# Block 0 of a bias-GELU MLP: a third pair of h columns by seven block products instead of eight

## The chip, the cores and the metric

The kernel runs on one core of a Trainium2 chip. The metric is device time in microseconds (us); "before" is a median of 875.78 us over 3 runs (875.62 to 875.81).

## The reference

```python
x  = (16, 512, 768)   # float32; taken as 8192 rows of 768
w1 = (768, 3072); b1 = (3072,); w2 = (3072, 768)
y = np.matmul(x, w1) + b1
y = 0.5 * y * (1.0 + erf(y / np.sqrt(2.0)))
return np.matmul(y, w2).astype(np.float32)
```

Two matrix products with a GELU between them. The kernel multiplies in bf16 and accumulates in fp32.

## The kernel before, in words

**Tiling.** The 8192 rows are taken in blocks of 2 x 384 rows (`pairs`; the last block is 2 x 256). The 3072 hidden columns are 24 chunks `hc` of 128. Chunk j and chunk 12 + j form pair j (j = 0 to 11). For each block the kernel makes `g = gelu(x w1 + b1)` in SBUF, one 128-column chunk of each half block at a time, and then the second product from `g`.

**First product, two ways.** `plain(hc, half)` (L407) makes one chunk of one half block with 6 matmuls 128x384 (L414); a pair has two chunks and two halves, so 24 matmuls. `product1` (L149) makes a pair with seven block products P1 to P7 of 3 matmuls each (L158), 21 in all, in the manner of Strassen and Winograd. It multiplies sums of blocks of w1 (seven forms per pair: two are copies of raw blocks, five are sums) with sums of blocks of x (`sum_x`, L296). Between the products VectorE and ScalarE work on the accumulators: after P1 a copy on ScalarE to a second bank, after P7 a copy to the buffer `v`, after P2 and after P6 a subtraction on VectorE (L114), and four GELUs on ScalarE (L146).

**The forms of w1.** `form_w1` (L400, through `make_w1`, L361) makes the forms of the next pair in the order `order1` = 4, 5, 3, 0, 1, 2, ...: a copy on ScalarE (L104) and four VectorE sums (L111, L114). They are kept in staging areas and later stored to DRAM (`w1f`), from which every later block loads them. In block 0 only pairs 4 and 5 are made by products; their forms are read where they were staged. All other pairs of block 0 are plain.

**Second product.** `part2` (L227, matmuls at L233) multiplies 128x128 blocks of `g` with forms of w2 (15 per chunk c of w2, c = 0 to 7) for 15 products M0 to M14 of 8 matmuls each, by groups of three row tiles (G0 and G1 in a block). `load_w2(c)` loads the six raw blocks of a chunk, and `make_w2(c)` (L331, from `w2_sums`, L314) makes the nine sums with six VectorE instructions, in place in `w2t[:, c]`. Sums of `g` that some products need are made by `gsum` (L191) on VectorE; `finish2` (L243) adds or copies each finished product from PSUM to `ot`.

In block 0 the second product of G0 starts with six products that need no sum of `g` (`raws`, L712), chunk by chunk: M4, M14, M13, M8, M7, M6 for c = 0, then for c = 1, up to c = 7. After them `middle` runs M12, M2, M1, M5, M3, M10, M9, M11, then M0. M5 needs a `gsum` of its own, made on VectorE just before. M4, M12, M10 and M11 share a PSUM bank (`BANK`): M11 adds to what M10 left, so it starts when VectorE has read M10's result.

**Borrowed space.** In block 0 the sums of x (`x0f`, L96) lie in `w2t[:, 7]` and the buffers `v` and `u` of the products (`ev0`, L97) lie in `w2t[:, 6]`. So `load_w2(6)` and `load_w2(7)` (L577) stand behind block 0's last product.

**What orders the work.** The order on every engine is the order of the program (`inorder`). VectorE's instructions are placed by hand between the TensorE steps, and each engine executes its own in order. Loads with conversion go through GpSimd's queue (`nc.gpsimd`): x tiles, w1 and w2 in the order in which they are written, with eight in flight (the ninth waits for the first). The next block's x tiles are loaded behind the w2 chunks on the same queue, and transposed from SyncE's queue (L294).

**The start and the end.** Before the first products TensorE runs matmuls on a zeroed tile (`busy`, L423) and transposes six tiles of x (`turn_x0`, L439). At the very end the last row tile is finished by three stretches of output columns (L761): 384, 192 and 192, each followed by a copy on ScalarE and a store from SyncE's queue.

Of the kernel before, what the change touches and what calls it, by code (L numbers as in the profile page):

```python
# [12 lines left out]
P = 128  # L13

W1F = {"P7": 0, "P1": 1, "P2": 2, "P3": 3, "P4": 4, "P6": 5, "P5": 6}
# [18 lines left out]
def kernel(  # L34
# [16 lines left out]
    HP = HC // 2  # L51
    KH = KC // 2
    NB = N // 2
    HW = 384
    QC = HC // 3
    QH = QC // 2
    SLOT = 7 * KH * P
# [7 lines left out]
    while r < R:  # L65
        w = min(HW, (R - r) // 2)
# [8 lines left out]
    def inorder(ins):  # L75
        return tc.keep_in_program_order(ins)
# [10 lines left out]
    w2t = keep.tile([P, QC, NF, NB], BF16, name="w2t")  # L87
# [14 lines left out]
    def copy(engine, dst, src):  # L102
        if engine == "act":
            inorder(nc.scalar.copy(out=dst, in_=src))  # L104
        elif engine == "dve":
            inorder(nc.vector.tensor_copy(out=dst, in_=src))  # L106
        else:
            inorder(nc.gpsimd.tensor_copy(out=dst, in_=src))

    def add(dst, a, b):  # L110
        inorder(nc.vector.tensor_tensor(out=dst, in0=a, in1=b, op=ALU.add))  # L111

    def sub(dst, a, b):
        inorder(nc.vector.tensor_tensor(out=dst, in0=a, in1=b, op=ALU.subtract))  # L114
# [14 lines left out]
    staged = {}  # L129
# [9 lines left out]
    def moving1(m, kc, w, xs):  # L139
        if m in XRAW:  # L140
            kh, half = XRAW[m]
            return xt[:, kh * KH + kc, half, :w]
        return xs[:, XF[m], kc, :w]
# [5 lines left out]
    def product1(t, m, p, j, w):  # L149
        if m == "P1":  # L150
            t["c12"] = bank()
        elif m == "P7":
            t["c22"] = bank()
        ps = t[{"P1": "c12", "P4": "c12", "P7": "c22", "P5": "c22"}.get(m, "c11")]
        at, xs, es = (staged[j], x0f, ev0) if p == 0 else (where[index(p, j)], xft, ev)
        forms = at.rearrange("p (f kc c) -> p f kc c", f=7, kc=KH)
        for kc in range(KH):
            inorder(nc.tensor.matmul(  # L158
                out=ps[:, :w], lhsT=forms[:, W1F[m], kc, :], rhs=moving1(m, kc, w, xs),
                start=(kc == 0 and m in ("P1", "P7")), stop=(kc == KH - 1),  # L160
                skip_group_check=True))
        ps = ps[:, :w]
        v, u = es[:, j % 2, :w], es[:, 2 + j % 2, :w]
        if m == "P1":
            t["c11"] = bank()
            copy("act", t["c11"][:, :w], ps)
        elif m == "P7":
            copy("dve", v, ps)
        elif m == "P2":
            sub(t["c22"][:, :w], ps, v)  # L170
        elif m == "P6":
            sub(u, ps, v)
        elif m == "P4":
            gelu1(HP + j, 0, ps, w, 1.0)
        elif m == "P3":
            if p > 0 and index(p, j) in places:
                fill_slot(places[index(p, j)])
            gelu1(j, 0, ps, w, 1.0)
        elif m == "P5":
            gelu1(j, 1, u, w, -1.0)  # L180
            gelu1(HP + j, 1, ps, w, -1.0)
# [128 lines left out]
    def load_w2(c):  # L310
        h, q = divmod(c, QH)
        dma(nc.gpsimd, out=w2t[:, c, 0:6, :].rearrange("p (k f) n -> p k (f n)", k=3), in_=w2r[:, h, q, :, :])
# [18 lines left out]
    def make_w2(c):  # L331
        for s in w2_sums(c):
            s()
# [17 lines left out]
    def raw(j):  # L351
        c0 = (j % 3) * P
        return w1_pair(j // 3).rearrange("p (b kc c) -> p b kc c", b=4, kc=KH)[:, :, :, c0:c0 + P]
# [4 lines left out]
    order1 = (4, 5, 3, 0, 1, 2, 6, 7, 8, 10, 11, 9)  # L358
    waiting = []

    def make_w1():  # L361
        nonlocal made
        n = made
        made += 1
        j = order1[n]
        a = raw(j)
        area, o = stage[n]
        s = area[:, o:o + SLOT].rearrange("p (f kc c) -> p f kc c", f=7, kc=KH)
        copy("act", s[:, 0:2], a[:, 1:3])

        def one():
            add(s[:, 2], a[:, 1], a[:, 2])
            add(s[:, 3:5], a[:, 0:4:2], a[:, 1:4:2])

        def two():
            sub(s[:, 5], a[:, 2], a[:, 0])
            sub(s[:, 6], a[:, 1], a[:, 3])
            if n < 4:
                waiting.append(lambda queue: dma(queue, out=w1f[j], in_=area[:, o:o + SLOT]))
            else:  # L380
                dma(nc.sync if n < 6 else nc.gpsimd, out=w1f[j], in_=area[:, o:o + SLOT])
            formed.add(j)
            staged[j] = area[:, o:o + SLOT]
            if j in DIRECT:
                where[seq.index(j)] = area[:, o:o + SLOT]

        return one, two
# [12 lines left out]
    def form_w1():  # L400
        for f in make_w1():
            f()
        free_slots()
# [3 lines left out]
    def plain(hc, half, k0=0, k1=KC):  # L407
        if k0 == 0:
            halfway[hc, half] = bank()
        py = halfway[hc, half]  # L410
        h, j = divmod(hc, HP)
        lhs = w1_group(j // 3 * 2 + h)
        for kc in range(k0, k1):
            inorder(nc.tensor.matmul(out=py[:, :HW], lhsT=lhs[:, kc, (j % 3) * P:(j % 3 + 1) * P],  # L414
                                     rhs=xt[:, kc, half, :], start=(kc == 0), stop=(kc == KC - 1)))
        if k1 == KC:
            gelu1(hc, half, py[:, :HW], HW, 1.0)
# [5 lines left out]
    def busy(n):  # L423
        for _ in range(n):
            inorder(nc.tensor.matmul(out=pw[:], lhsT=warm[:, 0:P], rhs=warm, start=True, stop=True))
# [77 lines left out]
    EARLY = ("M2a", "M3a")  # L503
# [3 lines left out]
    tb = turns[1][:, 448:448 + HC]  # L507
    inorder(nc.tensor.transpose(out=tb, in_=b1s, identity=ident32[:HC, :HC]))
    copy("act", b1t[:], tb)
    busy(2)  # L510
    copy("dve", xb0[:, 0, :], xw[:, 0, :])
    turn_x0(0, "dve")
    copy("act", xb0[:, 1, :], xw[:, 1, :])
    busy(1)
    turn_x0(1, "dve")
    busy(1)
    turn_x0(2, "dve")
# [18 lines left out]
    def plains(gi):  # L536
        for n in range(3):
            hc = gi % 2 * HP + gi // 2 * 3 + n
            plain(hc, 0)
            plain(hc, 1)  # L540

    blk = groups(0)
# [9 lines left out]
    form_w1()  # L552
    plain(3, 1)
    plain(HP + 3, 0)
    t0 = {4: dict(), 5: dict()}
    c0 = w2_sums(0)

    def step0(j, *ms):
        for m in ms:
            product1(t0[j], m, 0, j, HW)  # L560
# [13 lines left out]
    step0(5, "P4", "P6", "P5")  # L574
    plain(6, 0)
    step0(5, "P3")
    for c in (QC - 2, QC - 1):  # L577
        load_w2(c)
    for f in c0:
        f()  # L580
    form_w1()
    make_w2(1)
    plain(6, 1)
    for hc in (7, 8):
        plain(hc, 0)
        plain(hc, 1)
    for m in EARLY:
        gsum(blk[0], m)
    form_w1()
    make_w2(2)  # L590
    make_w2(3)
    make_w2(4)
    plains(5)
    for m in MIDDLE[:2]:
        gsum(blk[0], m)
    make_w2(5)
    make_w2(6)
    plains(6)
    plains(7)
    make_w2(7)  # L600
    for m in ("M1", "M3b", "M10a", "M10b", "M11a", "M11b"):
# [27 lines left out]
    for p, (r0, w) in enumerate(pairs):  # L629
        nxt = pairs[p + 1] if p + 1 < len(pairs) else None  # L630
        G0, G1 = blk
        blk = groups(p + 1) if nxt is not None else None
# [100 lines left out]
        if full:  # L733
            run(take(9))
            if p == 0:
                form_w1()
            for m in ("M14", "M8", "M4"):
                rest(G1, m)
            if p > 0:
                for k in range(4):  # L740
                    sum_x(k, nxt[1])
            for m in ("M7", "M6", "M13"):
                rest(G1, m)
            if p == 0:
                form_w1()
            at = {5: (0,), 6: (1,), 7: (2,)} if p == 0 else {}
            middle(G1, lambda n: [lambda k=k: sum_x(k, nxt[1]) for k in at.get(n, ())])
            if p > 0:
                ahead(p + 1)
            rest(G1, "M0")  # L750
            if p == 0:
                sum_x(3, nxt[1])
        else:
            a = lambda k: block(G1, 0, k)
            d12, d13 = st[:, 4, :, :], st[:, 5, :, :]
            sub(d12, a(0), a(1))
            sub(d13, a(0), a(2))
            t = ot[:, G1["o"][2], :]
            halves = ((("b31", a(2)), ("M4", a(1)), ("b11", d12)), (("M13", a(2)), ("b22", a(1)), ("b12", d13)))
            rows = of[G1["rows"][0]:G1["rows"][0] + P, :]  # L760
            for n, c0, c1 in ((0, 0, NB), (1, 0, NB // 2), (1, NB // 2, NB)):  # L761
                terms = halves[n]
                ps = bank()
                for f, lhs in terms:
                    for c in range(QC):
                        inorder(nc.tensor.matmul(  # L766
                            out=ps[:, :c1 - c0], lhsT=lhs[:, c, :], rhs=w2t[:, c, WF[f], c0:c1],
                            start=(f == terms[0][0] and c == 0), stop=(f == terms[2][0] and c == QC - 1)))
                o0, o1 = n * NB + c0, n * NB + c1
                copy("act", t[:, o0:o1], ps[:, :c1 - c0])  # L770
                dma(nc.sync, out=rows[:, o0:o1], in_=t[:, o0:o1])
# [30 lines left out]
```

## Time and profile before

| | us |
|---|---|
| median of 3 runs | 875.78 |
| the profiled execution: its own time | 876.35 |
| its span (first to last instruction) | 874.6 |
| TensorE (PE) busy | 868.5 (99%) |
| VectorE (DVE) busy | 593.2 (68%) |
| ScalarE (ACT) busy | 400.6 (46%) |
| GpSimd (POOL) busy | 86.0 (10%) |
| all that PE waited for others, in four waits | 2.8 |

The profile gives each engine's instructions with their start and duration in us from the start of the span. A timeline line holds the start, the duration, the engine, the line of the kernel, the operation, what it writes and reads, the shape, the count of merged instructions and, in brackets, the idle time before it and what ended that. The listed duration of an instruction holds its way through the engine as well; the next may start before it ends, so costs in a chain are taken from start to start. "PEld" is the loading of weights, which runs beside PE. Busy shares by stage, from the view of busy times in stretches:

| stretch, us | what PE does | DVE busy |
|---|---|---|
| 30.00 to 33.95 | last products of pair 5 | 2.57 of 3.95 |
| 33.95 to 38.80 | plain chunks | 4.75 of 4.85 |
| 38.80 to 47.50 | plain chunks | 8.46 of 8.70 |
| 47.50 to 56.40 | plain chunks | 7.60 of 8.90 |
| 56.40 to 64.20 | raw products of G0 | 7.59 of 7.80 |
| 64.20 to 73.30 | M12 to M9 of G0 | 8.99 of 9.10 |
| 73.30 to 83.00 | M11, M0, start of G1 | 9.31 of 9.70 |

### The profile page before, as it was taken

Reading aid. Unit: us, or ns where it says so; the run is one execution under the profiler, and the core shown is the slowest. Engines: PE = TensorE matmul, PEld = TensorE weight load, DVE = VectorE, ACT = ScalarE, POOL = GpSimd, SP = SyncE. Lnnn points to the kernel's source line nnn. Section 1 sums busy time; section 2 is a strip of 40 time slices with the busy share of each in tenths; the row PEclk is TensorE's granted clock in tenths of the full one; section 3 lists DMA queues with packets and bytes.
Section 4 is the critical chain, followed back from the end, with each engine's and each line's share of the span. In section 5 each row is a group of like instructions: output and inputs, shape, how many; then the busy total and the mean of one; then the engine's idle time right before and its main releaser. Section 6 shows DMA issues by size and latency. Waiting matters only on the chain.

```text
span 874.6 us, 14061 instructions
## 1 busy us (share of the span) xinstructions
PE 868.5 (99%) x5483; PEld 532.2 (61%) x5483; DVE 593.2 (68%) x1080; ACT 400.6 (46%) x794; POOL 86.0 (10%) x156
## 2 busy tenths in 40 slices
PE   8999999999999999999999999999999999999998
PEld 5666666666666666666666656666666666666775
DVE  3899868657755675676577556756765776577654
ACT  3742483167127614731671276147316712751560
POOL 6200110010110001000101100010001011000000
PEclk9999999999999999999999999999999999999999
DMA  9997698176627735671756277366717662771521
GB/s 190 207 217 241 223 323 222 73 216 205 158 66 240 201 91 161 212 169 73 228 196 154 76 233 205 84 170 205 172 69 229 197 152 79 234 194 55 197 80 73
DMA packets 89367, 148.00 MB, mean 169 GB/s; under 512 B 50876, under 2 KB 68436, under 8 KB 89300
## 3 DMA queue, kind: packets, MB, share of 16 engines
q1 hardware_dynamic: 64976, 97.04, 37.1%
q0 software_dynamic: 24144, 49.36, 23.5%
q8 instruction: 43, 0.70, 0.3%
q10 hardware_dynamic: 180, 0.70, 0.2%
q14 instruction: 24, 0.20, 0.1%
HBM read 123.88 MB, written 33.42 MB: 180 GB/s over the span
## 4 chain that ended last, share of the span: by engine, by line
PE 98%; DMA 1%; DVE 0%; POOL 0%; ACT 0%; issue 0%; DVEq 0%; ACTq 0%; POOLq 0%
PE ps L233 47%; PE ps L158 45%; PE ps L414 4%; PE ps L766 1%; DMA st<-in_x_dram 1%; PE ps L483 0%; POOL w1t L79 0%; DVE ps L114 0%; ACT g L146 0%; POOL st L79 0%; DVE ev L114 0%; PE ps L442 0%; DVE ev L106 0%; DVE g L114 0%; DVE st L114 0%
## 5 line engine op out<-in xcount | busy, mean ns | idle before, releaser
L158 PEld LDWEIGHTS <-w1t 128*128 128x128 bf16 x2436 | 238.3, 98 | 145.5 <-issue 1.1
L146 ACT ACTIVATE g<-ps,b1t 128x384 bf16<-128x384 f32 (+1 forms) x407 | 220.9, 570 | 87.9 <-PE ps L158 57.3
L158 PE MATMUL ps<-xft,w1t 128*128 128x384 bf16 (+1 forms) x1392 | 259.7, 320 | 0.0
L233 PE MATMUL ps<-w2t,g 128*128 128x384 bf16 x1512 | 257.6, 326 | 0.0
L233 PEld LDWEIGHTS <-g 128*128 128x128 bf16 x1512 | 147.9, 98 | 97.3
L158 PE MATMUL ps<-xt,w1t 128*128 128x384 bf16 (+1 forms) x1044 | 202.5, 320 | 0.2
L111 DVE TENSOR_TENSOR ot<-ot,ps 128x384 f32<-128x384 f32 x231 | 125.4, 552 | 106.3 <-PE ps L233 51.1
L233 PE MATMUL ps<-w2t,st 128*128 128x384 bf16 x1008 | 170.7, 326 | 0.0
L104 ACT COPY ot<-ps 128x384 f32<-128x384 f32 x129 | 61.0, 478 | 219.5 <-PE ps L233 199.3
L233 PEld LDWEIGHTS <-st 128*128 128x128 bf16 x1008 | 98.6, 98 | 65.2
L104 ACT COPY ps<-ps 128x384 f32<-128x384 f32 (+1 forms) x121 | 54.9, 454 | 132.7 <-PE ps L158 132.7
L114 DVE TENSOR_TENSOR ev<-ps,ev 128x384 f32<-128x384 f32 (+1 forms) x119 | 64.8, 544 | 74.9 <-PE ps L158 72.1
L114 DVE TENSOR_TENSOR ps<-ps,ev 128x384 f32<-128x384 f32 (+1 forms) x119 | 65.8, 553 | 44.5 <-PE ps L158 41.6
L106 DVE COPY ev<-ps 128x384 f32<-128x384 f32 (+1 forms) x119 | 64.4, 541 | 21.9 <-PE ps L158 21.6
L146 ACT ACTIVATE g<-ev,b1t 128x384 bf16<-128x384 f32 (+1 forms) x119 | 72.1, 606 | 15.3 <-DVE ev L114 15.3
L114 DVE TENSOR_TENSOR st<-g 128x1024 bf16<-128x1024 bf16 x107 | 72.9, 682 | 0.9 <-ACT g L146 0.9
L79 POOL DMA_DIRECT2D out_dram<-ot x60 | 32.6, 544 | 342.1 <-DVE ot L111 342.1
L114 DVE TENSOR_TENSOR g<-g 128x1024 bf16<-128x1024 bf16 x84 | 57.4, 684 | 0.4
L79 POOL DMA_DIRECT2D xb<-in_x_dram x38 | 20.6, 547 | 340.1 <-DMA xt<-xb 333.1
L414 PE MATMUL ps<-xt,w1t 128*128 128x384 bf16 x204 | 34.0, 326 | 0.0
L111 DVE TENSOR_TENSOR g<-g 128x1024 bf16<-128x1024 bf16 x42 | 29.0, 689 | 1.1
L111 DVE TENSOR_TENSOR st<-st,g 128x1024 bf16<-128x1024 bf16 x42 | 28.9, 687 | 0.8
(83 smaller groups left out, 265.4 us busy)
## 6 DMA issues: line engine op xcount, KB each, us to landing
w1t<-w1f SPq DMA_DIRECT2D x116, 672.0 KB, 5.3
out_dram<-ot POOLq DMA_DIRECT2D x60, 384.0 KB, 2.6
xb<-in_x_dram POOLq DMA_DIRECT2D x38, 192.0 KB, 4.4
w2t<-in_w_dram POOLq DMA_DIRECT2D x8, 576.0 KB, 21.7
ot<-in_x_dram POOLq DMA_DIRECT2D x18, 192.0 KB, 7.0
w1t<-in_w_dram POOLq DMA_DIRECT2D x4, 576.0 KB, 21.1
w1f<-st POOLq DMA_DIRECT2D x3, 672.0 KB, 4.4
w1f<-ot POOLq DMA_DIRECT2D x3, 672.0 KB, 8.8
```

Of the source, the lines that this page charges most:

```text
L79: inorder(queue.dma_start(out=out, in_=in_))
L104: inorder(nc.scalar.copy(out=dst, in_=src))
L106: inorder(nc.vector.tensor_copy(out=dst, in_=src))
L111: inorder(nc.vector.tensor_tensor(out=dst, in0=a, in1=b, op=ALU.add))
L114: inorder(nc.vector.tensor_tensor(out=dst, in0=a, in1=b, op=ALU.subtract))
L146: inorder(nc.scalar.activation(out=g[:, place_h(hc), half, :w], in_=src, func=ACTF.Gelu, bias=b1t[:, hc:hc + 1], scale=sign))
L158: inorder(nc.tensor.matmul(out=ps[:, :w], lhsT=forms[:, W1F[m], kc, :], rhs=moving1(m, kc, w, xs), start=(kc == 0 and m in ("P1", "P7")), ...
L233: inorder(nc.tensor.matmul(out=ps[:, :NB], lhsT=lhs[:, c, :], rhs=w2t[:, c, WF[m], :], start=(m in OPENS and c == 0), stop=(c == QC - 1), ...
L414: inorder(nc.tensor.matmul(out=py[:, :HW], lhsT=lhs[:, kc, (j % 3) * P:(j % 3 + 1) * P], rhs=xt[:, kc, half, :], start=(kc == 0), stop=(kc ...
L766: inorder(nc.tensor.matmul(out=ps[:, :c1 - c0], lhsT=lhs[:, c, :], rhs=w2t[:, c, WF[f], c0:c1], start=(f == terms[0][0] and c == 0), stop= ...
```

## The change

Pair 8 (chunks 8 and 20) of block 0 is made by `product1` in place of `plain`. Its five sums of w1 are made by a new function for this use alone, in free space of `w2t[:, 6]`; the forms that are stored for later blocks are still made in their turn. For all three pairs of block 0, P1 and P7 read the raw blocks of w1 in place of the copies, and the copy after P7 is on ScalarE and not on VectorE. Plain chunks change their order (7, 18 and 19 come ahead), so that 18, 19 and 9 lie around the products of pair 8. `load_w2(6)` and `load_w2(7)` move behind the products of pair 8. The `gsum` M3a moves behind a `form_w1`. At the start two zero matmuls ahead of `turn_x0(0)` go, and one more stands ahead of `turn_x0(1)`. At the end the last columns are 256 and 128.

```diff
-        forms = at.rearrange("p (f kc c) -> p f kc c", f=7, kc=KH)
+        forms = at.rearrange("p (f kc c) -> p f kc c", f=7, kc=KH)[:, W1F[m]]
+        if p == 0 and m in ("P7", "P1"):
+            forms = raw(j)[:, 1 + W1F[m]]
...
         elif m == "P7":
-            copy("dve", v, ps)
+            copy("act" if p == 0 else "dve", v, ps)
...
+    def sums(s, a):
+        add(s[:, 2], a[:, 1], a[:, 2])
+        add(s[:, 3:5], a[:, 0:4:2], a[:, 1:4:2])
+
+    def differences(s, a):
+        sub(s[:, 5], a[:, 2], a[:, 0])
+        sub(s[:, 6], a[:, 1], a[:, 3])
+
+    def form_once(j, area):
+        staged[j] = area
+        s = area.rearrange("p (f kc c) -> p f kc c", f=7, kc=KH)
+        sums(s, raw(j))
+        differences(s, raw(j))
...
-    busy(2)
     copy("dve", xb0[:, 0, :], xw[:, 0, :])
     turn_x0(0, "dve")
     copy("act", xb0[:, 1, :], xw[:, 1, :])
-    busy(1)
+    busy(2)
     turn_x0(1, "dve")
...
     step0(5, "P3")
-    for c in (QC - 2, QC - 1):
-        load_w2(c)
     for f in c0:
         f()
     form_w1()
     make_w2(1)
+    form_once(8, w2t[:, QC - 2].rearrange("p f n -> p (f n)")[:, 8 * HW:8 * HW + SLOT])
     plain(6, 1)
-    for hc in (7, 8):
+    for hc in (7, HP + 6):
         plain(hc, 0)
         plain(hc, 1)
-    for m in EARLY:
-        gsum(blk[0], m)
+    gsum(blk[0], EARLY[0])
+    step0(8, "P1", "P7")
+    plain(HP + 7, 0)
+    step0(8, "P2", "P4")
     form_w1()
+    plain(HP + 7, 1)
+    step0(8, "P6", "P5")
+    plain(9, 0)
+    step0(8, "P3")
+    for c in (QC - 2, QC - 1):
+        load_w2(c)
+    gsum(blk[0], EARLY[1])
     make_w2(2)
     make_w2(3)
     make_w2(4)
-    plains(5)
     for m in MIDDLE[:2]:
         gsum(blk[0], m)
     make_w2(5)
     make_w2(6)
-    plains(6)
+    plain(9, 1)
+    for hc in (10, 11):
+        plain(hc, 0)
+        plain(hc, 1)
     plains(7)
     make_w2(7)
...
-            for n, c0, c1 in ((0, 0, NB), (1, 0, NB // 2), (1, NB // 2, NB)):
+            for n, c0, c1 in ((0, 0, NB), (1, 0, 2 * P), (1, 2 * P, NB)):
```

More of the change, by code (lines that the diff above doesn't have):

```diff
@@ L155, in product1 @@
         at, xs, es = (staged[j], x0f, ev0) if p == 0 else (where[index(p, j)], xft, ev)
-        forms = at.rearrange("p (f kc c) -> p f kc c", f=7, kc=KH)
+        forms = at.rearrange("p (f kc c) -> p f kc c", f=7, kc=KH)[:, W1F[m]]
+        if p == 0 and m in ("P7", "P1"):
+            forms = raw(j)[:, 1 + W1F[m]]
         for kc in range(KH):
             inorder(nc.tensor.matmul(
-                out=ps[:, :w], lhsT=forms[:, W1F[m], kc, :], rhs=moving1(m, kc, w, xs),
+                out=ps[:, :w], lhsT=forms[:, kc, :], rhs=moving1(m, kc, w, xs),
                 start=(kc == 0 and m in ("P1", "P7")), stop=(kc == KH - 1),
@@ L371, in one @@
         def one():
-            add(s[:, 2], a[:, 1], a[:, 2])
-            add(s[:, 3:5], a[:, 0:4:2], a[:, 1:4:2])
+            sums(s, a)
         def two():
-            sub(s[:, 5], a[:, 2], a[:, 0])
-            sub(s[:, 6], a[:, 1], a[:, 3])
+            differences(s, a)
             if n < 4:
@@ L554 @@
     plain(HP + 3, 0)
-    t0 = {4: dict(), 5: dict()}
+    t0 = {4: dict(), 5: dict(), 8: dict()}
     c0 = w2_sums(0)
```

## The prediction

> **What bounds the kernel now.** I read the waits of PE first: they say what PE, busy 99% of the span, ever stood still for (us in total, times, longest).
>
> ```profile
> PE ps L425 <- DVE st L454: 1.2, 1, 1.2
> PE ps L442 <- DMA st<-in_x_dram: 1.0, 1, 1.0
> PE ps L483 <- DVE xt L106: 0.4, 2, 0.2
> PE ps L442 <- ACT st L104: 0.2, 1, 0.2
> ```
>
> All four lie in the first 13 us. After that PE never waits: each matmul more or less is time, and so is each new wait, for nothing later can absorb it. The chain of waits in order of time gives the start's limit and PE's pace:
>
> ```profile
> 5.44 6.75 DMA st<-in_x_dram
> ...
> 34.11 22.43 PE ps L414 x138
> 56.54 39.00 PE ps L233 x240
> ```
>
> A tile of x lands at 12.19, and PE starts on it at 12.24; what PE does before is cover. 22.43/138 = 0.1625 us is one 128x384 matmul. Then VectorE's timeline between the edit and its deadlines:
>
> ```profile
> 32.20 0.56 DVE L114 TENSOR_TENSOR w2t<-ps,w2t 128x384 f32<-128x384 f32 x1 [0.84 <-PE ps L158]
> ...
> 34.59 0.82 DVE L111 TENSOR_TENSOR ev<-xft 128x384 bf16<-128x384 bf16 x2
> 35.33 0.62 DVE L114 TENSOR_TENSOR ev<-xft 128x384 bf16<-128x384 bf16 x2
> 35.87 0.55 DVE L111 TENSOR_TENSOR w2t<-w2t 128x768 bf16<-128x768 bf16 x1
> ...
> 48.56 0.56 DVE L111 TENSOR_TENSOR w2t<-w2t 128x768 bf16<-128x768 bf16 x1 [1.06 <-DMA w2t<-in_w_dram]
> ...
> 67.00 0.68 DVE L111 TENSOR_TENSOR st<-g 128x1024 bf16<-128x1024 bf16 x1
> ...
> 71.66 1.47 DVE L111 TENSOR_TENSOR ot<-ot,ps 128x384 f32<-128x384 f32 x3
> ```
>
> From 32.20 to beyond 73 VectorE has one gap: it waits for a w2 chunk until 48.56. So it is the second bound, just behind PE. PE's timeline shows how close:
>
> ```profile
> 64.17 5.36 PE L233 MATMUL ps<-w2t,st 128*128 128x384 bf16 x32
> 69.37 1.46 PE L233 MATMUL ps<-w2t,g 128*128 128x384 bf16 x8
> 70.67 2.76 PE L233 MATMUL ps<-w2t,st 128*128 128x384 bf16 x16
> 73.27 10.56 PE L233 MATMUL ps<-w2t,g 128*128 128x384 bf16 x64
> ```
>
> The first line is M12, M2, M1, M5, 8 matmuls (1.30 us) each, so M5 starts at 68.07; its sum (VectorE's line at 67.00) is done at 67.68. M11 starts at 73.27; the third addition of the line at 71.66 reads M10 out of the bank that M11 needs, and ends at 71.66 + 1.47 = 73.13: 0.14 ahead.
>
> **The change, part by part.**
>
> *PE.* Pair 8 takes 21 matmuls and not 24: 3 x 0.1625 = **-0.49 us**. With the plain chunks starting at 33.95, P2 of pair 8 starts 42 matmuls later at 40.78, P6 12 later at 42.73, and the second product 135 later at 55.89 (now 56.37).
>
> *VectorE, from 32.20.* Nothing ahead of it moves, for it waits for P6 of pair 5. Added until the deadlines: the five sums of pair 8, from start to start 1.28 us (35.87 - 34.59, the same four instructions), and two subtractions from PSUM of 0.47 to 0.48 each (from the one at 32.20 to the next at 32.67). The removed P7 copies lay at 26.35 and 29.76, where PE's products set the pace: worth nothing.
> Now the queue in its new order. `make_w2(1)` ends at 38.85 as now; the five sums end at 40.13, M2a (0.71, 38.85 to 39.56) at 40.84. Then VectorE must wait for P2: pairs 4 and 5 show a subtraction 0.74 us after the start of P2's matmuls and 0.69 after P6's. So P2's starts at 41.52; behind it `form_w1` (1.28) ends at 43.28, and P6's starts at 42.73 + 0.69 = 43.42. Plus 0.47, plus M3a (0.61, 39.56 to 40.17): `make_w2(2)` starts at 44.50 and not 41.45, which is 3.05 late. The one gap gives back 1.15 (from the end of `make_w2(3)`, 44.43 + 2.98 = 47.41, to 48.56). **VectorE is 1.90 us late** from there on, at one `make_w2` per 2.98 us without a gap.
>
> *What is late next.* M14 of chunk 7 needs the fifth instruction of `make_w2(7)`, done at 61.52 now, 63.42 then; PE is there at 55.89 + 43 x 0.1625 = 62.88: a wait of 0.6. M5's sum is done at 67.68 + 1.90 = 69.58; with 0.05 for the signal (7.72 to 7.77 in PE's wait on L106) and 0.16 for the weights (PEld runs so far ahead of PE) M5 starts at 69.79 and not 68.07: +1.72. M11 may start at 73.13 + 1.90 + 0.05 = 75.08 and not 73.27: **+1.81**, the -0.49 included. Behind it M0 needs M9's addition (ends 74.19 now, M0 starts 74.57): 76.09 against 76.38, no wait. G1's first such places have over 1 us (M5 of G1: sum ends 86.38, PE at 87.57).
>
> *ScalarE.* Three P7 copies and one P1 copy more, 0.46 each. Between GELUs it idles 0.39 per 0.975 us. The copy for pair 5 pushes the GELU at 29.87 to about 30.25, the free time at 30.95 to 31.22 takes it up: 0. Without that cover a bank would come free 0.4 late, eight banks behind: still 0. Raw blocks for P1 and P7 take away a wait that PE doesn't have: 0.
>
> *GpSimd's queue.* `load_w2(6)` now waits for pair 8's GELU (about 44.6, was 33.3), `load_w2(7)` for its P3 (45.4, was 34.9); behind them stand four x tiles (37.4 to 46.3, then from 46.2), and SyncE's transposes (first at 58.02) wait for those. Loads land in turn 2.8 to 3.1 us apart: the one at 28.86 took 22.5 and landed at 51.4, so the queue is never empty at 45, and chunks 6 and 7 land at 54.2 and 57.0 as now. VectorE wants them at 57.6 and 60.6: 0, with 3.4 us of cover. x tiles land as now; VectorE reads them first at 92.15.
>
> *Start.* `turn_x0(0)` may come 0.3 us earlier; `turn_x0(1)` starts at 6.07 because ScalarE's cast ends at 6.01, behind a DMA; all of it ends in the wait for the tile that lands at 12.19. Between a loss that the 1.0 us of wait covers and no gain: 0.
>
> *End.* The pace of 192 columns is 1.98/24 = 0.0825 us, and durations grow from 219 ns (128) over 246 (192) to 273 (256): two equal steps, so 256 + 128 costs PE what 192 + 192 does. The last ScalarE copy goes from 0.32 us toward 0.27 (by 24 columns at 0.18 and 384 at 0.48): -0.05. The last store carries 64 KB and not 96: the 96 KB moved in about 0.43 us and 384 KB in about 0.97, so 0.0019 per KB, -0.06; if by bytes alone -0.14, if by rows (128 in both) 0. I take **-0.11**, between -0.05 and -0.19.
>
> **Sum:** 1.81 - 0.11 = +1.70. The profiled execution took 876.35 (span 874.6), so 878.05 beside it; against the median, 875.78 + 1.70 = **877.5**.
>
> **The rivals.**
> 1. *VectorE doesn't wait for pair 8* (its 0.17 + 0.66 us of waits fall away, say because PSUM signals sooner): D = 2.24 - 1.15 = 1.09, time 876.7. Against it: these lags repeat four times in pairs 4 and 5.
> 2. *Not slower at all.* M11's place decides: PE waits 1 us for each us that VectorE is late beyond 0.09 (0.14 less the signal). If the added sums hide wholly, PE keeps its -0.49 and the end's -0.11: 875.2. This would need VectorE 0.4 us earlier than now with 2.24 us more to do and 1.15 of gap. Nothing in the rows does that.
> 3. *The late loads land late.* They meet a shorter queue and a busy VectorE. If their descriptors were written only once VectorE stands still, at 57.6, chunk 6 comes 0.75 (issue) + 2.9 (transfer) later: +3.7, 881.2. Against it: the load issued at 34.88, with VectorE busy 4.75 of 4.85 us, landed after about 22 us like the one at 25.97 (22.6); GpSimd's x issues took 0.53 to 0.57 in that stage and 0.55 at the start, VectorE idle. The Trainium skill, "SBUF — State Buffer", at its warning on the "DVE blocks DMA" trap, says that a DMA from GpSimd's queue can't get its descriptors written while VectorE holds the port that both share; these rows don't show it for the sums here.
> 4. *The new standstill slows PE's clock.* 1.6 us at M5, 0.6 before it. At half pace for 3.4 us that is 1.7 more: 879.2. Against it: after the 1.0 us wait at 12.24 the granted clock stays 1.00. The Trainium skill, "TensorE: Matmul & The Clock Gate", in "Why this matters for your kernels", allows gaps up to about 3 us; 1.6 us is not shown here.
>
> **Chances.** Forecast 0.70 (877.5 +- 0.3), rival 1 0.12, rival 2 0.06, rival 3 0.04, rival 4 0.03, another late wait of VectorE or ScalarE 0.03, an early gain that no row shows 0.02. The bound of 0.2% (1.75 us, about what a measurement of this kernel can tell from no change) is 877.53, in the middle of the forecast: I split it evenly. Within: 0.35 + 0.12 + 0.06 = 0.53; slower: 0.35 + 0.04 + 0.03 + 0.03 = 0.45; faster 0.02. The range goes from below rival 1 (876.4) to the forecast with an unseen wait of about 1 us (878.6).
>
> **What would show it.** Right: three new waits of PE between 60 and 76 us, for VectorE, some 2.3 us together; `make_w2(2)` near 44.5; no gap on VectorE near 48; the second product from 55.9; the last store's copy under 0.3 us. Wrong: VectorE idle between 45 and 67 (then a load or PE sets the pace), PE waiting before 55, or M5 starting before 69.

## The result and the profile after

The changed kernel takes 878.16 us (median of 6 runs, 877.98 to 879.8) against 875.65 beside it (875.2 to 875.81): ratio 1.0035, 95% interval 1.0022 to 1.0048. It is slower by 2.5 us. The forecast was +1.7, so the direction and the mechanism that I gave are there, but 0.8 us more came with them. Three later measurements of the same program gave +2.9 to +3.1 (878.69 - 875.56, 878.79 - 875.85, 878.76 - 875.70). Single runs far off all others (1139.6, 1009.5 and 5272 us) are left out of what follows.

The waits of PE in the changed kernel's profile (us in total, times, longest):

```profile
PE ps L160 <- DMA w1t<-w1f: 2.1, 2, 1.3
PE ps L235 <- DVE st L111: 1.3, 1, 1.3
PE ps L439 <- DVE st L468: 1.2, 1, 1.2
PE ps L235 <- DVE w2t L114: 0.5, 1, 0.5
PE ps L497 <- DVE xt L106: 0.4, 2, 0.2
PE ps L160 <- DVE ps L114: 0.3, 1, 0.3
PE ps L456 <- ACT st L104: 0.2, 1, 0.2
```

Four of the seven rows are new. The two at L235 are second products of block 0: the ones that I forecast. The two at L160 (first products, once waiting for w1 forms from DRAM and once for VectorE) lie in block 1, where I had looked for nothing. Their places, from PE's timeline (start, duration, shape; in brackets the idle time and what ended it):

```profile
62.30 0.97 PE L235 MATMUL ps<-w2t,g 128*128 128x384 bf16 x5 [0.48 <-DVE w2t L114]
63.11 4.06 PE L235 MATMUL ps<-w2t,st 128*128 128x384 bf16 x24
68.42 1.47 PE L235 MATMUL ps<-w2t,st 128*128 128x384 bf16 x8 [1.25 <-DVE st L111]
...
73.86 2.44 PE L235 MATMUL ps<-w2t,g 128*128 128x384 bf16 x14
```

```profile
105.67 0.65 PE L160 MATMUL ps<-xt,st 128*128 128x384 bf16 x3 [0.29 <-DVE ps L114]
...
124.23 1.15 PE L160 MATMUL ps<-xft,w1t 128*128 128x384 bf16 x6 [0.85 <-DMA w1t<-w1f]
...
129.09 1.15 PE L160 MATMUL ps<-xft,w1t 128*128 128x384 bf16 x6 [1.27 <-DMA w1t<-w1f]
```

The row at 62.30 is M14 of chunk 7, 68.42 is M5 and 73.86 is M11. M11 has no wait in brackets, but M10 and M9 start at 71.03, and 71.03 + 16 x 0.1625 = 73.63: it comes 0.23 late. VectorE's timeline, with P2's subtraction of pair 8, the starts of `make_w2(2)` and `make_w2(3)`, M5's sum and the three additions ahead of M11:

```profile
40.31 0.57 DVE L114 TENSOR_TENSOR ps<-ps,w2t 128x384 f32<-128x384 f32 x1 [0.72 <-PE ps L160]
...
43.26 0.55 DVE L111 TENSOR_TENSOR w2t<-w2t 128x768 bf16<-128x768 bf16 x1
...
46.24 0.55 DVE L111 TENSOR_TENSOR w2t<-w2t 128x768 bf16<-128x768 bf16 x1
...
67.68 0.68 DVE L111 TENSOR_TENSOR st<-g 128x1024 bf16<-128x1024 bf16 x1
...
72.33 1.47 DVE L111 TENSOR_TENSOR ot<-ot,ps 128x384 f32<-128x384 f32 x3
```

The wait of 0.72 for P2 is there, the gap near 48 us is gone, and M5's sum (67.68) and the three additions (72.33) each come 0.7 later than before in this profile, with the first plain matmul 1.22 earlier (15.18, not 16.40): 1.9 late, as forecast.

To tell where the time came from I cut each profiled execution at five starts of PE's timeline. The first column, the start of the first plain matmul, differs between executions of one and the same program. From there on the pieces repeat, except that to block 1's second product.

| us | first plain matmul at | to M11 | to the plain chunk behind block 0 | to block 1's second product | to the last row tile | to the end | sum behind the first column |
|---|---|---|---|---|---|---|---|
| before | 16.40 | 56.87 | 22.10 | 41.03 | 727.06 | 11.12 | 858.18 |
| changed, five executions | 15.18 to 16.86 | 58.68 to 58.70 | 22.10 | 41.45 to 43.88 | 727.23 to 727.25 | 10.96 to 10.99 | 860.45 to 862.84 |

So block 0 costs +1.82 (forecast +1.81) and the end gives 0.15 back (forecast 0.11). What the forecast did not have is block 1, with 0.42 to 2.85, and the long middle, with 0.18. (One of the five is the kernel with the old start, below.)

### The profile page after: what moved, and what is told of

Read it like the earlier page. It is cut to its first block, busy times and chain, and to the rows that moved or that the text cites. A ratio compares the mean times of both kernels' runs of the same rounds, so it can differ in the third digit from the quotient of the medians.

```text
span 878.0 us, 14062 instructions
## 1 busy us (share of the span) xinstructions
PE 868.8 (99%) x5479; PEld 531.3 (61%) x5479; DVE 594.3 (68%) x1084; ACT 401.9 (46%) x798; POOL 85.8 (10%) x156
## 4 chain that ended last, share of the span: by engine, by line
PE 93%; DVE 4%; DMA 2%; ACT 0%; issue 0%; SPq 0%; DVEq 0%; ACTq 0%
PE ps L235 45%; PE ps L160 44%; PE ps L428 2%; DVE w2t L114 2%; DMA w1t<-w1f 1%; PE ps L789 1%; PE ps L497 1%; DVE ot L111 0%; DMA ot<-in_x_dram 0%; DVE st L114 0%; DVE g L114 0%; DVE w2t L111 0%; DVE ps L114 0%; DVE st L111 0%; PE ps L456 0%
## 5 line engine op out<-in xcount | busy, mean ns | idle before, releaser
L160 PEld LDWEIGHTS <-w1t 128*128 128x128 bf16 x2442 | 238.7, 98 | 148.7 <-DMA w1t<-w1f 2.9
L160 PE MATMUL ps<-xft,w1t 128*128 128x384 bf16 (+1 forms) x1392 | 259.8, 320 | 2.1 <-DMA w1t<-w1f 2.1
L235 PE MATMUL ps<-w2t,g 128*128 128x384 bf16 x1512 | 257.8, 326 | 0.5 <-DVE w2t L114 0.5
L235 PEld LDWEIGHTS <-g 128*128 128x128 bf16 x1512 | 147.9, 98 | 98.2 <-issue 1.0
L160 PE MATMUL ps<-xt,w1t 128*128 128x384 bf16 (+1 forms) x1044 | 202.5, 320 | 0.2
L235 PE MATMUL ps<-w2t,st 128*128 128x384 bf16 x1008 | 170.8, 326 | 1.3 <-DVE st L111 1.3
L235 PEld LDWEIGHTS <-st 128*128 128x128 bf16 x1008 | 98.5, 98 | 66.7 <-DVE st L111 1.6
L428 PE MATMUL ps<-xt,w1t 128*128 128x384 bf16 x180 | 30.7, 326 | 0.0
```

What stands on the lines that cost most here:

```text
L160: inorder(nc.tensor.matmul(out=ps[:, :w], lhsT=forms[:, kc, :], rhs=moving1(m, kc, w, xs), start=(kc == 0 and m in ("P1", "P7")), stop=(kc ...
L235: inorder(nc.tensor.matmul(out=ps[:, :NB], lhsT=lhs[:, c, :], rhs=w2t[:, c, WF[m], :], start=(m in OPENS and c == 0), stop=(c == QC - 1), ...
```

## The experiments

### Each part of the change alone

**Start and end alone**: the kernel before with the moved zero matmuls and the last columns 256 and 128.

```diff
-    busy(2)
     copy("dve", xb0[:, 0, :], xw[:, 0, :])
...
-    busy(1)
+    busy(2)
...
-(1, 0, NB // 2), (1, NB // 2, NB)
+(1, 0, 2 * P), (1, 2 * P, NB)
```

> Before, with the start and the end of the changed kernel alone: the moved zero matmuls and the last columns 256+128. Theory 1 (VectorE's lateness in block 0 makes the loss): the start gives 0, for it ends in the wait for a tile of x, the end gives -0.15 (ScalarE's last copy 0.27 for 0.32 us, and 0.10 less from that copy to the end of the span): 875.5. Rival A (the moved zero matmuls cost the 0.8 us by which the loss is larger than forecast): 876.3.

Measured 875.69 against 875.56, ratio 1.0000 (0.9991 to 1.0009). **The changed kernel again, and with the old start** (only the zero matmuls put back):

> The changed kernel once more. Its six runs lay at 878.0 to 878.2 (four) and at 879.7 to 879.8 (two, the profiled one among them). Theory 1: in each run the three waits of PE for VectorE between 60 and 76 us, some 2.3 us together, M11 1.81 us later beside the end of the start than before; the 2.1 us of waits for w1 forms from DRAM in block 1 come in the runs near 879.8 alone. Rival B: waits for the w1 forms are in every run, some 0.8 us in those near 878.1, and make up what the forecast lacked.

> The changed kernel with the zero matmuls where they were. Theory 1: as the changed kernel beside it, within 0.2 us. Rival A (the moved zero matmuls cost 0.8 us): 0.8 us less than the changed kernel beside it.

878.69 (1.0033, 1.0020 to 1.0046) and 878.90 (1.0036, 1.0023 to 1.0048): the start is worth nothing that can be told.

**Everything but pair 8**: the kernel before with the start, the end, the raw blocks for P1 and P7, and P7's copy on ScalarE.

```diff
+        if p == 0 and m in ("P7", "P1"):
+            forms = raw(j)[:, 1 + W1F[m]]
...
-            copy("dve", v, ps)
+            copy("act" if p == 0 else "dve", v, ps)
```

> Before, with all of the change but pair 8: raw blocks for P1 and P7 and P7's copy on ScalarE for pairs 4 and 5, the moved zero matmuls, the last columns 256+128. Theory 1: 0 from all but the end, -0.16 from that: 875.4. Rival A: the start or ScalarE's copies cost what the forecast lacked: 876.4.

875.63 against 875.81, ratio 0.9998 (0.9989 to 1.0007). So the whole rise belongs to pair 8 and to what moves with it (the order of the plain chunks, `load_w2(6)` and `load_w2(7)`, M3a).

Its trace shows one thing more: to M11 it takes 57.49, 0.61 more than before. Its first plain matmul starts 1.30 earlier (15.10), but the w2 chunk for which VectorE waits lands only 0.56 earlier, and the three additions ahead of M11 come only 0.60 earlier (71.06). So VectorE is 0.70 late against PE; 0.09 of that is covered at M11, and PE loses the rest. An early start is thus in part lost where VectorE waits for that chunk. In the changed kernel this gap is used up, and to M11 it takes 58.68 to 58.70 with starts from 15.18 to 16.86. The +1.82 is therefore the price against a start near 16.4; against one as early as 15.10 it would be about 1.2 (an estimate: 58.69 - 57.49).

**Pair 8's sums without pair 8**: the kernel before, with the five sums made three times into free space and not used, behind `make_w2(1)`.

```diff
     make_w2(1)
+    for _ in range(3):
+        a = raw(8)
+        add(spot[:, 2], a[:, 1], a[:, 2])
+        add(spot[:, 3:5], a[:, 0:4:2], a[:, 1:4:2])
+        sub(spot[:, 5], a[:, 2], a[:, 0])
+        sub(spot[:, 6], a[:, 1], a[:, 3])
     plain(6, 1)
```

> Before, with the five sums of w1 for pair 8 made three times over on VectorE behind the second make_w2, and used by nothing: VectorE alone gets more work, 3 x 1.28 = 3.84 us. Theory 1: less the gap of 1.15 us VectorE is 2.69 us late, less the 0.09 us at M11 the kernel is 2.6 us slower: 878.3. Rival C (VectorE's added work is hidden; the loss comes from the later loads or the changed order): 875.7.

877.86 against 875.56: +2.3, ratio 1.0024 (1.0014 to 1.0034). The trace shows the same waits at M14 and M5 with no third pair at all:

```profile
63.70 0.97 PE L233 MATMUL ps<-w2t,g 128*128 128x384 bf16 x5 [0.73 <-DVE w2t L114]
...
69.83 1.47 PE L233 MATMUL ps<-w2t,st 128*128 128x384 bf16 x8 [1.26 <-DVE st L111]
```

From the first plain matmul to M11 it takes 59.42, +2.55 against 2.60 forecast. The price of block 0 is VectorE's lateness, whatever makes it late. In block 1 this kernel has none of the new waits (41.02), though VectorE was later still. So those waits don't come from lateness.

### VectorE's work in the order of PE's deadlines

If only the places at M14, M5 and M11 cost, another order of the same VectorE work should save them. **First order:** the sums behind `make_w2(7)` in the order of use, and the additions of M7, M6, M5, M2 and M3 held back to M10 and later. As I wrote it, two row tiles are stored before some of their terms are added: one leaves out M2, the other M6 and M5.

> The changed kernel, with VectorE's work in block 0 set in the order of its deadlines: M12's and M2's sums of g behind the last make_w2, the sums of M5, M10, M9, M11 and M0 and the additions that open a PSUM bank again ahead of the additions that nobody waits for (M7, M6, M2, M5, M3). The same work in another order. Theory 1 (the new waits come from VectorE being 1.90 us late where there was 0.09 us of room): PE's three waits in block 0 go, M11 starts 2.3 us earlier against the end of the start than in the changed kernel; against before the kernel gains 0.49 + 0.16 us and pays what the new waits in block 1 cost (0.42 us fixed, and 0 to 2.4 for w1 forms): 875.3 to 877, by theory 2 (these belong to the instructions' place in the stream and not to the lateness). If they come from the lateness, they go too: 874.9.

885.64, ratio 1.0102 (1.0086 to 1.0117; forecast 875.3 to 877). Block 0's waits before 75 us are gone (56.67 to M11), but VectorE then stands still for a store, as its timeline shows:

```profile
81.04 1.02 DVE L111 TENSOR_TENSOR ot<-ot,ps 128x384 f32<-128x384 f32 x2 [6.92 <-DMA out_dram<-ot]
```

The held additions write into rows that are being sent. That is my order's mistake, and says nothing of pair 8. **Second order:** each held addition ahead of its row's store. And the same with twelve tiny writes at VectorE's start, for the question of the next part.

```diff
-    for m in ("M1", "M3b", "M10a", "M10b", "M11a", "M11b"):
+    for m in ("M12", "M2b", "M1", "M3b"):
         gsum(blk[0], m)
...
+            by_deadline(G0, (("M12", ("M5",), ("M10a", "M10b")), ("M2", (), ()), ("M1", (), ("M9a", "M9b")),
+                             ("M5", (), ("M11a", "M11b")), ("M3", (), ()), ("M10", (), ("M0a", "M0b")),
+                             ("M9", (), ()), ("M11", (), ())), held, lambda m: [])
```

> Edit: the changed kernel, whole, with VectorE's work from 55 to 93 us in the order in which TensorE wants it: behind make_w2(7) the sums for M12, M2, M1, M3, then M5's sum, then M10's, M9's, M11's and M0's; the additions of M7 and M6 and both of M5 only behind M10's (but ahead of the stores of their rows); in G1 M5's sum ahead of form_w1 and M0's sums and M10's addition earlier. Not one instruction more or less on any engine. Theory (the five sums of pair 8 and its two subtractions cost only because they make VectorE 1.9 us late at M14, M5 and M11 of G0): no wait of TensorE between 55 and 80, M11 starts 56.4 to 56.7 after the first plain matmul (before 56.87, changed 58.69), M11 to the first matmul of block 1 stays 22.10 if G1 has room, and the time is that of before less 0.49 (three matmuls) and 0.16 (end) plus what block 1 costs (0.42, and up to 1 us of w1-form loads): 875.0 to 876.2. Rival (VectorE's work is a bound of its own up to the end of G1, so the lateness is only moved): waits of 0.5 to 1.8 us appear at M5 or M11 of G1, 82 to 93 us, and the time stays above 876.8.

> Edit: the kernel with VectorE in deadline order, plus the twelve tiny writes at VectorE's start. If the wait behind P2 in block 1 (0.42) goes with the place in VectorE's stream, its trace has no wait for VectorE's subtraction near 104 us, and the time is 0.2 to 0.4 below that of the deadline order alone (less than these medians can tell alone): 874.8 to 876.0. If the wait has another cause it is there again.

878.47 (1.0031, 1.0019 to 1.0044; forecast 875.0 to 876.2) and 878.52 (1.0032, 1.0019 to 1.0045; forecast 874.8 to 876.0). M11 comes 56.39 after the first plain matmul, but M0 then waits in both groups:

```profile
74.79 9.26 PE L235 MATMUL ps<-w2t,g 128*128 128x384 bf16 x56 [1.83 <-DVE ot L111]
...
95.05 1.46 PE L235 MATMUL ps<-w2t,g 128*128 128x384 bf16 x8 [0.60 <-DVE ot L111]
```

M0 needs M9's addition, as the prediction had said, and I had put the held additions ahead of it. These two waits, 2.4 us, are what the wrong order costs. On the twelve writes the pair says nothing: in the second order the wait behind P2 in block 1 is gone without them as well, for the new order had already changed the place of that subtraction among VectorE's instructions. **Third order:** M9's addition first; M3's addition is held back too, and the first sums of x come later.

```diff
-            finish2(G, m, held if m == "M5" else None)
+            finish2(G, m, held if m in ("M5", "M3") else None)
...
-            if m == "M10":
+            if m == "M9":
                 run(held)
...
-                at = {"M10": 0, "M9": 1, "M11": 2}
+                at = {"M9": (0, 1), "M11": (2,)}
```

> Edit: the deadline order of before, mended where it made TensorE wait: M9's addition (which M0 waits for) now stands ahead of the held additions of M7, M6, M5 and M3 in G0, and ahead of the first sums of x in G1. The same instructions as the changed kernel, in another order on VectorE. Theory (the pair costs only by VectorE's place in the queue at single deadlines): no wait of TensorE between 55 and 96 us above 0.2; first plain matmul to M11 56.4, to the plain chunk behind block 0 78.5 (before 78.97, changed 80.77); the time that of before less 0.65, plus 0 to 1.3 for the loads of w1 forms in block 1: 874.9 to 876.3. Rival (VectorE's sum of work bounds block 0): the 2.4 us of waits come back at another place before 96 us and the time stays above 877.5.

```profile
55.26 7.96 PE L235 MATMUL ps<-w2t,g 128*128 128x384 bf16 x48
63.06 5.36 PE L235 MATMUL ps<-w2t,st 128*128 128x384 bf16 x32
68.26 1.46 PE L235 MATMUL ps<-w2t,g 128*128 128x384 bf16 x8
69.56 2.76 PE L235 MATMUL ps<-w2t,st 128*128 128x384 bf16 x16
72.16 10.62 PE L235 MATMUL ps<-w2t,g 128*128 128x384 bf16 x64
```

These 168 matmuls follow each other without a wait at M14, M5, M11 or M0. It is 56.39 to M11 (0.48 less than before: the three matmuls) and 78.77 to the plain chunk behind block 0, against 78.97 before and 80.78 changed. So VectorE's sum of work does not bound block 0; its order did. The time came down by less, to 877.33 (1.0018, 1.0009 to 1.0027; forecast 874.9 to 876.3), because this trace spends 42.81 and not 41.03 in block 1.

### The waits of block 1

**VectorE's late instruction.** VectorE's timeline in the changed kernel, around P2's second subtraction in block 1:

```profile
103.99 0.55 DVE L106 COPY ev<-ps 128x384 f32<-128x384 f32 x1
105.05 0.57 DVE L114 TENSOR_TENSOR ps<-ps,ev 128x384 f32<-128x384 f32 x1 [0.51 <-PE ps L160]
```

The record of its semaphore wait ends at 104.63, and it starts at 105.05. In the kernel before the record of the wait ends at 104.05, and the subtraction follows at 104.09:

```profile
104.09 0.57 DVE L114 TENSOR_TENSOR ps<-ps,ev 128x384 f32<-128x384 f32 x1
```

Counted from 0 with the semaphore records, the late instruction is VectorE's number 191. Other starts late by 0.4 behind a wait that had ended are number 1215 in the changed kernel (750.85 us), 831 and 959 in the one before (507.52 and 589.20), 703 and 831 in the one with everything but pair 8: each is 63 plus a multiple of 128. To move the number, twelve tiny writes go to VectorE's start:

```diff
+    for _ in range(12):
+        inorder(nc.vector.memset(ev[:, 0, 0:2], 0.0))
```

> The changed kernel with 12 more VectorE instructions (memsets of two elements) in its idle start. Theory 2 (the 0.42 us at which PE waits for VectorE's subtraction after P2 in block 1, in all three traces of the changed program, comes from the place of that instruction in VectorE's stream; the same delay of 0.4 us stands in before at 507 us): the wait at this place goes, 0.42 us less than the changed kernel, if the place where it moves to is covered. Rival D: it stays, for the work ahead of it is the same.

The late start is gone. Time 877.94 (1.0023, 1.0014 to 1.0033), still with 0.8 us of waits for w1 forms; the 0.42 alone is too little to be told in these medians.

**The late w1 forms.** In block 1 SyncE issues several loads of w1 forms (672 KB each), the first three close behind each other. In the changed kernel one 16 KB packet of the instruction queue q8 falls among their first. The DMA view of 118.0 to 119.0 us:

```profile
q1 hardware_dynamic: 8, 0.04, 17.4%
q8 instruction: 1, 0.02, 5.9%
```

PE has 5479 matmuls and as many weight loads, and q8 moved 43 packets, one for 255 of them; so I took q8 to feed PE with instructions. Then an edit to PE's stream should move its packets, and the table below shows that it does. To shift them, 19 one-column matmuls stand at the start in place of two zero matmuls (34 instructions more):

```diff
-    busy(7)
+    for _ in range(19):
+        inorder(nc.tensor.matmul(out=pw[:, :1], lhsT=warm[:, 0:P], rhs=warm[:, :1], start=True, stop=True))
+    busy(5)
```

> The changed kernel with 19 matmuls of one column in place of two of the first seven zero matmuls: 17 matmuls and 17 weight loads more in PE's stream of instructions, so that its 16 KB fetches of instructions come some 3 us earlier against its work. In before and in the kernel with three-fold sums such a fetch lies 19.0 us behind block 1's first plain matmul, in the changed kernel 22.0 to 22.4, where PE's loads of w1 forms begin to be late. Theory 2 (the place of instruction fetches decides how the loads of w1 forms and GpSimd's store and x loads meet): the waits for w1 forms in block 1 go to under 0.1 us and VectorE's 0.42 us stays: 877.6. Rival D (the loads meet by chance, or by the lateness): waits of 0 to 2.4 us as before, 878.2 to 878.9.

The waits for w1 forms were gone in the trace, but the median was 878.69 (1.0029, 1.0018 to 1.0040), and not the 877.6 that I expected: by itself no proof. So the same shift was set on the third order, and both shifts on the changed kernel, with the changed kernel beside it.

> Edit: the mended deadline order, and at the start nineteen one-column matmuls in place of two of the first seven zero matmuls, which moves TensorE's later instructions by 34 places in its stream. If the waits for w1 forms in block 1 go with the place at which TensorE's instructions are fetched, its trace has none of them and the time is that of before less 0.65 in most runs: 874.6 to 875.4, and 0.3 to 1 below the order alone. If they come from GpSimd's loads of x meeting SyncE's, they are there again and the two times agree within 0.3.

876.41 (1.0008, 0.9999 to 1.0017; forecast 874.6 to 875.4), 0.92 below the order alone on the same chip, with no wait for a w1 form.

> Edit: the changed kernel with both shifts at once: twelve tiny writes on VectorE and nineteen one-column matmuls in place of two zero matmuls at the start. Block 0 is untouched, so its 1.81 stays. If the rest of the rise is the two waits of block 1, both are gone in the trace (first plain matmul behind block 0 to the first second-product matmul of block 1: 41.0 to 41.1, not 41.5 to 43.9) and the median comes down to the forecast's sum: that of before plus 1.6 to 2.0, 877.2 to 877.8, and 0.4 to 1.2 below the changed kernel on this chip. If the rise is elsewhere, the two agree within 0.3.

> The changed kernel again, without an edit, as the measure for the other run on this chip: 878.0 to 878.9 (878.16 and 878.69 so far).

879.0 (1.0036, 1.0023 to 1.0049) beside 878.79: not lower, against the expectation. On this chip the kernel before spread over 2 us as well, and no trace of the run shows whether the waits were there. Once more:

> The kernel with both shifts, once more, for a trace that can be read and a median. If the rise beyond 1.7 lies in the two waits of block 1: from the first plain matmul behind block 0 to block 1's second product 41.0 to 41.1 us (41.45 to 43.9 in the changed kernel), and a median 0.4 to 1.2 below the changed kernel's on this chip. If the trace has no such waits and the medians agree within 0.3, the waits in the one profiled execution aren't what sets the median.

> The changed kernel without an edit beside it: 878.0 to 878.9 again, with the wait of 0.42 behind P2 in block 1.

877.86 (1.0025, 1.0016 to 1.0034) beside 878.76 (1.0036, 1.0023 to 1.0050): 0.90 lower. Its waits of PE hold the two of block 0 and none of block 1:

```profile
PE ps L235 <- DVE st L111: 1.3, 1, 1.3
PE ps L523 <- DVE ev L470: 1.2, 1, 1.2
PE ps L456 <- DVE st L106: 0.8, 1, 0.8
PE ps L235 <- DVE w2t L114: 0.5, 1, 0.5
PE ps L499 <- DVE xt L106: 0.2, 1, 0.2
```

Block 1 takes 41.02 in it, as before. Fifteen traces (all that can be read but that of the first order), counted from the plain chunk behind block 0:

| | q8's packet at | SyncE's third load issued after the second by | block 1, us |
|---|---|---|---|
| before, its sums thrice, everything but pair 8 | 19.1, 19.1, 19.7 | 0.82 | 41.02 |
| the three with PE's stream shifted | 18.8 to 19.4 | 0.81 to 0.82 | 41.02 to 41.39 |
| changed, five executions | 22.0 to 22.4 | 1.16 to 1.58 | 41.45 to 43.88 |
| twelve writes; second order, with and without them; third order | 21.7 to 22.3 | 1.36 to 1.48 | 42.21 to 42.80 |

SyncE's first load of these is issued at 21.5 to 21.9 and its second 0.37 later. Where the packet falls on them, the third is issued 0.3 to 0.8 later than the 0.82 of the other traces; where it comes 2 us ahead, never. GpSimd issues a store of w1 forms 0.4 us behind SyncE's first load: in the traces with the late third issue that store lands at 29.3 to 30.2 and SyncE's second load at 30.7 to 33.1; in the six others the store lands at 30.8 to 31.2 and the load at 28.7 to 29.2. So GpSimd's transfers go ahead of SyncE's there. That packet, issue and landing go together is shown by moving the packet three times; how one 16 KB packet holds SyncE's loads up is not shown.

How long PE then waits goes with something else: the first column. With the packet among the loads, PE's waits for w1 forms are 0 and 0.14 us in the two traces whose first plain matmul starts at 16.2 or later, and 0.8 to 2.1 in the seven that start at 15.8 or earlier. The three traces with PE's stream shifted all start at 16.2 or later. So their missing waits alone would not tell the shift from a late start; the landings do, for those of the two late starts are late as well. Why an early start makes the waits longer is not shown.

## Why the prediction was right, and where it fell short

- *PE, -0.49*: right. The third order, with no wait, is 0.48 shorter to M11.
- *VectorE 1.90 late*: right. P2's wait was 0.72 (0.66 forecast), `make_w2(2)` started at 43.26, which is 28.08 behind the first plain matmul (44.50 - 16.40 = 28.10 forecast), and the gap near 48 was used up. Rival 1 fell with that. The 1.15 of that gap was, however, the figure of one execution: in the kernel with everything but pair 8, whose trace starts earlier, VectorE waits 1.80 there and not 1.06.
- *M14 0.6, M5 +1.72, M11 +1.81*: M14 waited 0.48; M5 came 53.24 behind the first plain matmul and not 51.67, +1.57, so that the 0.16 that I added for weights was not needed; M11 +1.81 to +1.83. Behind M11 nothing more in block 0: 22.10 in both. Rival 2 named M11 as the place that decides, and the third order shows that: VectorE in time there, and PE keeps its three matmuls.
- *GpSimd's loads, 0*: right. Chunks 6 and 7 landed at 54.05 and 56.86 (54.2 and 57.0 forecast), issued at 43.70 and 44.44 with VectorE at work, and there is no gap in `make_w2` from 43 to 62 us. Rival 3 fell: the warning of the Trainium skill that I named there ("SBUF — State Buffer") is not seen for these bf16 sums.
- *Clock, rival 4*: fell. The eight matmuls of M5 behind 1.25 us of standstill take 1.31 us (68.42 to 69.73), so they keep 0.16 us each.
- *Start, 0*: right as a price (875.69 against 875.56), wrong as an explanation. I said that it "ends in the wait for the tile that lands at 12.19". That wait of 1.0 stands only in the one profiled execution of before. The first plain matmul lies anywhere from 15.0 to 16.9 in these traces, and no edit of the start tells in the medians. That the price is right is therefore luck in part.
- *End, -0.11*: measured -0.15; the last copy takes 0.27, as forecast.
- **The failed step** is the sum itself: "another late wait of VectorE or ScalarE" got a chance of 0.03, and I priced everything behind M0 at nothing, since PE had no wait there before. Two terms were missing: the late VectorE instruction in block 1 (0.42 in every trace of the changed kernel) and the w1 forms (block 1 longer by a further 0 to 2.43). The 0.18 of the long middle is missing as well; with the twelve tiny writes alone it takes 726.87 and not 727.24, so it hangs on late starts too. Neither the late instruction nor the w1 forms come of VectorE's lateness: the kernel with thrice the sums is later still and has neither. With the two instruction streams moved, the trace has neither; for the w1 forms the start plays a part too, as said above. In time the move was worth 0.90 on one chip and nothing that could be told on another. The 0.90 leaves +2.2 by medians, and +1.46 from the first plain matmul to the end in the trace (58.68 + 22.10 + 41.02 + 726.86 + 10.98 = 859.64, before 858.18).
- With the forecast of 877.5 only 0.03 under the bound of 877.53, these 0.4 to 2.9 us carried the time across: "within", to which I gave 0.53, was wrong. Of the forecast's own part, block 0 and the end, the mechanism was right.

What stays open: how much of the 0.7 between those medians and that trace is the start, which differs by more than that from one execution to the next; and why the third order with PE's stream shifted, whose trace is as long as that of before behind the first plain matmul (858.23 and 858.18), keeps none of its 0.48: 0.29 go between M11 and block 1, 0.31 in block 1, where waits for VectorE of 0.23 (at M11 of G1) and 0.16 can be seen. No version beat the kernel before; the one with everything but pair 8 equals it.

## What to carry to other kernels

Three matmuls of a pair were to be had for five sums and two subtractions on another engine, but that engine was 0.14 us ahead at one bank, so each of its late microseconds was one of PE's. Before work is added to an engine that is not the bound (VectorE was busy 68%), find the deadlines that it meets narrowly; and if it must be added, put its queue in the order of those deadlines, with each addition ahead of whoever waits for its bank or its row. And where PE has no slack, an edit also shifts the places of all later instructions in their streams, and with them late starts and loads a block further on: that was 0.4 to 2.9 us in block 1 here, and the range needs room for it. Where one profile is all there is, a wait in its first microseconds, or a gap that ends with a load, may be that execution's alone.

## What the runs showed of the hardware

- **Late starts on VectorE by place.** The six late instructions named above, all with the number 63 plus a multiple of 128, started 0.4 us after their waits had ended; number 191 did so in each of the five executions of the changed kernel, and twelve instructions more took the late start off that place. The profile's queue q14 moved 24 instruction packets, 0.20 MB in all, 8 KB each. The Trainium skill, "Runtime: NRT & Kernel Launch", "Instruction fetch mechanics", says that an engine's instructions are refilled in blocks of 16 KiB, 256 instructions, so 64 bytes each, and that crossing a block is mostly hidden. For PE the size agrees (q8: 43 packets, 0.70 MB). By 64 bytes, q14's 8 KB are 128 instructions, the spacing of the late starts; that this queue feeds VectorE is not shown. If the late starts are such crossings, which is not shown either, they were not hidden: 0.42 here.
- **PE's instruction packet and SyncE's loads.** With the packet at their issue, the third load was issued 1.16 to 1.58 us behind the second and not 0.82, the second landed at 30.7 to 33.1 and not at 28.7 to 29.2, and PE waited 0 to 2.1 us for w1 forms in block 1; with the packet 2 us earlier it never did, in six traces of six.
- **A standstill of 1.25 us** of PE left the next matmuls at full pace: eight in 1.31 us, with a granted clock of 1.00.
